# Weight parts at another remainder of 256 bytes than activations, in a two-layer trunk on one core

## The chip, the core and the metric

The kernel runs on one core of a Trainium2 chip. A core has a matrix engine (TensorE: PE in the profile, its weight loads PEld), a vector engine (VectorE, DVE), a scalar engine (ScalarE, ACT), GpSimd (POOL) and a queue engine (SyncE, SP) that here only starts transfers. Operands lie in SBUF, an on-chip memory of 128 partitions; an address in this document is a byte offset within each partition. A matmul loads a 128 x 128 block (the stationary operand, `LDWEIGHTS` in the profile) and then passes another block of 128 rows and up to 512 columns through it (the moving operand, `MATMUL`); the result goes to PSUM. The metric is the time of one execution in microseconds, the median of several runs.

## What is computed

Two decoder layers on a sequence of 512 tokens, width 2048, in float32: a retention layer (8 heads) and a latent attention layer (16 heads), each behind an RMS norm that is scaled and shifted by a conditioning vector, each with a gate path, then a last RMS norm.

```python
def reference(x, c, positions, ada_w, ada_b, norm_g, ret_w_in, ...):
    c_act = jax.nn.silu(c)
    for i in range(DEPTH):                      # DEPTH = 2
        mod = (c_act @ ada_w[i] + ada_b[i])[:, None, :]
        shift, scale, gate = jnp.split(mod, 3, axis=-1)
        h = rmsnorm(x, norm_g[i]) * (1.0 + scale) + shift
        if i % N_MIXERS == 0:
            y = retention_branch(h, positions, ...)    # (silu(g) * y) @ w_out
        else:
            y = mla_branch(h, positions, ...)          # (silu(g) * o) @ w_out
        x = x + gate * y
    return rmsnorm(x, final_norm_g)
```

## The kernel before

**Parts.** Every float32 operand of the large products is split in two tiles of a faster matmul type: a high part (ACT copies it into the type) and a low part (DVE subtracts the high part from the original). One product is then three matmuls: high by high, high by low, low by high. In the profile `vg_03o_h` and `vg_03o_l` are the two parts of one weight tile. Nearly all of the 11,100 matmul records are of this type.

**Stages, in order of time.** The opening forms the normed input `hT` and the first head's q, k, v and gate together (line 409). Then, head by head for the retention layer: v and gate weights of heads 1 to 7 (`vg`, lines 806 to 808, `seven_steps`), and between them q and k of heads 2 to 5 (`qk_..`, line 905, `seven_rows_steps`); q and k of heads 1, 6 and 7 go through `mm3` (lines 163 to 165). The retention itself runs beside the output projection (`o`, line 1387). The second layer has a gate product (`g`, lines 163 to 165 and 1651), the latent rows (`vgc`, `seven_steps` again), two gate groups (`g_..`, line 905 again), attention with its up-projections (`uq`, `uk`, `uv`, `a`, `o<-pt,v`), and the last projection (`o_w`, lines 163 to 165 and 2309).

**Which side the weights are on.** In `seven_steps` (function `product`, line 801 on) and in the first head's `v`, the block of the activations is loaded and the weights, 512 columns wide, move. Everywhere else that `whi` and `wlo` tiles are used, the weights are loaded and the activations move, 512 columns wide in most stages and 256 wide in the two `seven_rows_steps` families, in line 1651 and in the last halves of the output projections. A `seven_steps` block has 8 steps of 4 forms and 8 of 3, each form 2 x 3 matmuls: 336 matmuls; a `seven_rows_steps` group has 4 steps of 4 forms and 4 of 3, each form 12 matmuls: also 336.

**Where tiles lie.** The pool `base` is open all the time. A tile without a tag, or a tag with all its buffers, gets its place when its first tile is created, each new one behind the last. The pools `l0`, `lp`, `l1`, `l2` follow one another in the space behind `base`. Sizes are rounded to 32 bytes. The memory map of the kernel before is:

| what | first address | remainder of 256 |
|---|---|---|
| `ident`, `mask`, `ones`, `mhalf`, `rt` | 4224 | 128 for the first |
| `spacer` (32 bytes) | 5824 | 192 |
| `vcol` (736 bytes) | 5856 | 224 |
| `a_col0`, `a_col1`, `b_col0`, `b_col1`, `gate_c0`, `gate_c1` (64 bytes each) | 6592 | 192 for the first |
| `big` (16 tiles of 4096: `hT`, `h2`, inputs of the output projections, heads' q, k, v) | 6976 | 64 |
| `small` (24 of 32) | 72512 | 64 for the first |
| `k4` (8), `k4b` (4), `tmp` (6 of 2048), `raw` (3): `sums` 0 to 11, latent parts, staging | 73280 | 64 |
| `whi` (3), `wlo` (3): high and low parts of most weights | 147008 | 64 |
| `qn_s`, `mod_c` | 171584 | 64 |
| pools `lp`, `l1`, `l2` begin | 171776 | 0 |
| `lp`: `sums` 12 to 15 (activations) | 188160 | 0 |
| `lp`: `own_h`, `own_l` (weights) | 204544 | 0 |
| `l2`: `bm` (weights in `vgc` and `g_..`) | 220928 | 0 |

All these large tiles have row lengths that are multiples of 512 bytes, and every matmul operand starts at a multiple of 512 bytes within its tile, so an operand has its tile's remainder of 256.

`turns` (line 782 on) deals the weight tiles out: of every four pairs of parts, three are in `whi`/`wlo` and one in the pool's own tiles. With the counts of this kernel the own tiles always get the same steps: `vg_01o`, `03o`, `05o`, `07o`, `11e`, `13e`, `15e`, `17e`, and `qk_01o`, `03o`, `11e`, `13e`. The `sums` 12 to 15 serve the forms s and y of steps 6 and 7 (of `vg`; steps 3 of `qk`).

**Order.** The order of instructions on each engine is written out by hand (`queued`, `behind`); the change leaves it as it is.

Of the kernel before, what the change touches and what calls it, by code (L numbers as in the profile page):

```python
# [9 lines left out]
F32 = mybir.dt.float32  # L10
# [6 lines left out]
P = 128  # L17
T = 512
NT = T // P
D = 2048  # L20
KD = D // P
# [28 lines left out]
def hybrid_trunk_kernel(  # L50
# [26 lines left out]
    PE, ACT, DVE, POOL = nc.tensor, nc.scalar, nc.vector, nc.gpsimd  # L77
# [5 lines left out]
    base = ctx.enter_context(tc.tile_pool(name="base", bufs=1))  # L83
# [38 lines left out]
    mhalf = base.tile([P, NT], F32, name="mhalf")  # L122
    DVE.memset(mhalf, -0.5)
    rt = base.tile([P, 4], F32, name="rt")
    spacer = base.tile([P, 8], F32, name="spacer")
    DVE.memset(spacer, 0.0)

    def rsqrt(src, n, mul, name):

# [91 lines left out]
    gate_bias = (vcol[:, 136:152], vcol[:, 152:168])  # L221
    final_c = vcol[:, 168:184]

    a_col = [base.tile([P, KD], F32, name=f"a_col{i}") for i in range(2)]
    b_col = [base.tile([P, KD], F32, name=f"b_col{i}") for i in range(2)]
    gate_c = [base.tile([P, KD], F32, name=f"gate_c{i}") for i in range(2)]

    def modulate(i, ps_shift, ps_scale, k0, n):

# [193 lines left out]
    @contextmanager  # L423
    def behind(*engines):

        with ExitStack() as stack:
            for e in engines:
                ins = next((i for i in reversed(nc.cur_bb.bb.instructions) if i.engine == e), None)
                if ins is not None:
                    stack.enter_context(tc.issue_after(ins))  # L430
            yield

    def queued(fn, *args):
        with behind(A_, V_, T_, S_):
            return fn(*args)
# [186 lines left out]


    queued(sum_mod, 0, 0, 1)
    low_v = queued(prepares["v", 0])
    for half in range(2):
        queued(sum_mod, 0, 1, half)
# [154 lines left out]
    def turns(raw_tags, part_tags):  # L782

        n = [0, 0]

        def raw_tile(shape, name):
            n[0] += 1
            pool, tag, bufs = raw_tags[n[0] % len(raw_tags)]
            return pool().tile(shape, F32, tag=tag, bufs=bufs, name=f"{name}_r")

        def part_tiles(shape, name):
            n[1] += 1
            pool, tags, bufs = part_tags[n[1] % len(part_tags)]
            return [pool().tile(shape, F32R, tag=tag, bufs=bufs, name=f"{name}_{p}") for p, tag in zip("hl", tags)]

        return raw_tile, part_tiles
# [943 lines left out]
            DVE.tensor_add(latent["q"][2 + b], m4[b], y_[b])  # L1740
            DVE.tensor_add(latent["kv"][2 + b], m5[b], y_[b])

    qn_s = base.tile([P, 16], F32, name="qn_s")[:, :NT]

    def latent_norm(n):
        if n == "q":
# [410 lines left out]
    for i, step in enumerate(steps):  # L2157
# [8 lines left out]
        with behind(S_):  # L2166
# [3 lines left out]
            if i in (n_p, n_l2):  # L2170
                pool, tables, n0 = (pools["l1"], rotary, 0) if i == n_p else (pools["l2"], rotary2, 2)
# [301 lines left out]
```

## Time and profile before

| | us |
|---|---|
| median of 3 runs | 2152.52 |
| lowest and highest | 2151.73, 2153.0 |
| the profiled execution | 2153.75 |
| its span, first to last instruction | 2151.9 |

The profile is of one execution. Busy time of PE is the time in which at least one matmul record is open; matmuls overlap in the records, so that what a matmul costs in a row of matmuls is the step from its start to the start of the next. Where the text needs that step it is taken from the timeline: the starts of the first matmul and of the matmul behind the last, divided by the number between them. A name such as `z<-vg_03o_h,hT` reads: written tile, then the moving operand and the loaded one in the order of their names; `x2` behind a row is two matmuls merged in one row.

### The profile page before, as it was taken

Reading aid. Unit: us, or ns where it says so; the run is one execution under the profiler, and the core shown is the slowest. Engines: PE = TensorE matmul, PEld = TensorE weight load, DVE = VectorE, ACT = ScalarE, POOL = GpSimd, SP = SyncE. Lnnn points to the kernel's source line nnn. Section 1 sums busy time; section 2 is a strip of 40 time slices with the busy share of each in tenths; the row PEclk is TensorE's granted clock in tenths of the full one; section 3 lists DMA queues with packets and bytes.
Section 4 is the critical chain, followed back from the end, with each engine's and each line's share of the span. In section 5 each row is a group of like instructions: output and inputs, shape, how many; then the busy total and the mean of one; then the engine's idle time right before and its main releaser. Section 6 shows DMA issues by size and latency. Waiting matters only on the chain.

```text
span 2151.9 us, 30042 instructions
## 1 busy us (share of the span) xinstructions
PE 2128.1 (99%) x11100; PEld 1822.9 (85%) x11100; DVE 1675.4 (78%) x2482; ACT 1056.5 (49%) x1604; POOL 106.8 (5%) x178
## 2 busy tenths in 40 slices
PE   8999999999999999999999999999999999999998
PEld 5888898988889888888888888898889989888887
DVE  7898788888878789766777787667978788886745
ACT  5764444444444444434444435345446565664434
POOL 1010000000000000000000000010001000000000
PEclk9999999999999999999999999999999999999999
DMA  9975687877777778755646566553556544346734
GB/s 388 398 279 192 218 277 226 277 238 261 256 259 259 232 231 288 250 193 177 244 148 239 188 212 246 166 174 112 166 181 211 185 129 147 117 134 222 243 108 137
DMA packets 229783, 462.96 MB, mean 215 GB/s; under 512 B 20818, under 2 KB 84338, under 8 KB 225794
## 3 DMA queue, kind: packets, MB, share of 16 engines
q1 hardware_dynamic: 217424, 421.85, 59.5%
q0 software_dynamic: 11920, 38.91, 4.6%
q8 instruction: 87, 1.43, 0.3%
q14 instruction: 62, 0.50, 0.1%
q10 hardware_dynamic: 290, 0.27, 0.0%
HBM read 417.96 MB, written 43.00 MB: 214 GB/s over the span
## 4 chain that ended last, share of the span: by engine, by line
PE 84%; DVE 6%; DMA 5%; issue 2%; ACT 2%; POOL 1%; SPq 0%; DVEq 0%; POOLq 0%; ACTq 0%
PE o L1387 11%; PE o L2309 4%; PE y L807 2%; PE y L806 2%; PE y L808 2%; PE s L807 2%; PE s L806 2%; PE x L807 2%; PE x L806 2%; PE s L808 2%; PE x L808 2%; PE x_qk L905 2%; PE s_qk L905 2%; PE y_qk L905 2%; PE qk L165 2%
## 5 line engine op out<-in xcount | busy, mean ns | idle before, releaser
L1387 PE MATMUL o<-o_h,o_whi 128*128 128x512 f32 (+1 forms) x496 | 192.3, 388 | 0.0
L1387 PE MATMUL o<-o_h,o_wlo 128*128 128x512 f32 (+1 forms) x496 | 192.1, 387 | 0.2 <-DVE o_wlo L138 0.2
L1387 PE MATMUL o<-o_l,o_whi 128*128 128x512 f32 (+1 forms) x496 | 191.4, 386 | 0.0
L1387 PEld LDWEIGHTS o<-o_h,o_wlo 128*128 128x128 f32 x496 | 93.1, 188 | 20.8 <-DVE o_wlo L138 2.0
L138 DVE TENSOR_TENSOR o_wlo<-o_r,o_whi 128x1024 fp32r<-128x1024 f32 x61 | 74.5, 1223 | 44.9 <-ACT o_whi L137 41.4
L1387 PEld LDWEIGHTS o<-o_l,o_whi 128*128 128x128 f32 x496 | 93.2, 188 | 18.4
L1387 PEld LDWEIGHTS o<-o_h,o_whi 128*128 128x128 f32 x496 | 93.2, 188 | 18.1
L165 PE MATMUL qk<-hT,qk_l 128*128 128x512 f32 x192 | 75.5, 393 | 1.5 <-DVE qk_l L138 1.5
L163 PE MATMUL qk<-hT,qk_h 128*128 128x512 f32 x192 | 75.8, 395 | 0.0
L164 PE MATMUL qk<-hT,qk_h 128*128 128x512 f32 x192 | 75.2, 392 | 0.0
L1089 DVE SCALAR_TENSOR_TENSOR mod<-mod,c_odd 128x1024 f32<-128x1024 f32 x48 | 58.0, 1220 | 21.4 <-DMA mod<-in_ada_t_dram 21.4
L358 DVE SCALAR_TENSOR_TENSOR aw<-aw,c_all 128x2048 f32<-128x2048 f32 (+1 forms) x35 | 73.1, 2102 | 1.8 <-DMA aw<-in_ada_t_dram 1.6
L137 ACT CAST o_whi<-o_r 128x1024 fp32r<-128x1024 f32 x61 | 63.5, 1051 | 22.4 <-PE o L1387 14.3
L138 DVE TENSOR_TENSOR o_w_lo<-o_w_raw,o_w_hi 128x1024 fp32r<-128x1024 f32 x32 | 38.9, 1219 | 33.3 <-ACT o_w_hi L137 33.2
L1089 DVE SCALAR_TENSOR_TENSOR mod<-mod,c_bm 128x1024 f32<-128x1024 f32 x48 | 58.5, 1218 | 0.0
L2309 PE MATMUL o<-o_h,o_w_hi 128*128 128x512 f32 (+1 forms) x160 | 55.6, 348 | 0.0
L2309 PE MATMUL o<-o_h,o_w_lo 128*128 128x512 f32 (+1 forms) x160 | 55.5, 347 | 0.0
L2309 PE MATMUL o<-o_l,o_w_hi 128*128 128x512 f32 (+1 forms) x160 | 55.4, 347 | 0.0
L1242 ACT ACTIVATE yn<-y,nmr,gn_r 128x512 f32<-128x512 f32 x32 | 22.3, 778 | 62.0 <-DVE nmr L1236 62.0
L137 ACT CAST o_w_hi<-o_w_raw 128x1024 fp32r<-128x1024 f32 x32 | 33.5, 1050 | 36.9 <-PE o L2309 33.1
L164 PE MATMUL o<-o_l,o_w_hi 128*128 128x512 f32 x128 | 50.0, 391 | 0.7 <-DVE o_l L138 0.6
L137 ACT CAST o_h<-o_in 128x1024 fp32r<-128x1024 f32 x24 | 25.2, 1051 | 51.3 <-PE o L164 47.6
(1608 smaller groups left out, 6893.4 us busy)
## 6 DMA issues: line engine op xcount, KB each, us to landing
mod<-in_ada_t_dram SPq DMA_DIRECT2D x96, 512.0 KB, 6.0
o_r<-in_ret_w_out_dram SPq DMA_DIRECT2D x64, 512.0 KB, 5.3
aw<-in_ada_t_dram SPq DMA_DIRECT2D x30, 1024.0 KB, 8.9
mod_gate<-in_ada_t_dram SPq DMA_DIRECT2D x32, 512.0 KB, 5.4
o_w_raw<-in_mla_w_out_dram SPq DMA_DIRECT2D x32, 512.0 KB, 4.0
qk_r<-in_ret_w_in_dram SPq DMA_DIRECT2D x48, 256.0 KB, 3.1
qk_r<-qk_d SPq DMA_DIRECT2D x32, 256.0 KB, 5.5
v_r<-v_d SPq DMA_DIRECT2D x32, 256.0 KB, 6.1
```

The costliest lines, as they stand in the source:

```text
L137: ACT.copy(hi, src)
L138: DVE.tensor_sub(lo, src, hi.bitcast(F32))
L163: PE.matmul(o, lhs[0], rhs[0], start=first and not seeded, stop=False, skip_group_check=seeded)
L164: PE.matmul(o, lhs[0], rhs[1], start=False, stop=False, skip_group_check=seeded)
L165: return PE.matmul(o, lhs[1], rhs[0], start=False, stop=last, skip_group_check=seeded)
L806: PE.matmul(banks[b], a[0], w[0], start=first, stop=False, skip_group_check=True)
L807: PE.matmul(banks[b], a[0], w[1], start=False, stop=False, skip_group_check=True)
L808: PE.matmul(banks[b], a[1], w[0], start=False, stop=True, skip_group_check=True)
L905: PE.matmul(o, w[wp][:, i, b * P : (b + 1) * P], a[ap], start=first and i + b + k == 0, stop=k == 2, skip_group_check=True,)
L1089: DVE.scalar_tensor_tensor(out=aw, in0=aw, scalar=1.0, in1=silu_c[j], op0=ALU.mult, op1=ALU.mult, accum_out=mc[:, j, b : b + 1],)
L1387: PE.matmul(o, w[i][:, ki, c0 + b * P : c0 + (b + 1) * P], a[j], start=first and i + j == 0, stop=last and i == 1, skip_group_check=True,)
L2309: PE.matmul(banks2[b][:, cols], w[0][i][:, 0, b * P : (b + 1) * P], o2_moving(w, u, cols)[j], start=u + i + j == 0, stop=u == KD - 1 and i ...
```

## The change

The diff moves tiles; it adds and removes no work but one small fill.

```diff
@@ -122,8 +122,6 @@
     rt = base.tile([P, 4], F32, name="rt")
-    spacer = base.tile([P, 8], F32, name="spacer")
-    DVE.memset(spacer, 0.0)
@@ -221,9 +219,9 @@
-    a_col = [base.tile([P, KD], F32, name=f"a_col{i}") for i in range(2)]
-    b_col = [base.tile([P, KD], F32, name=f"b_col{i}") for i in range(2)]
-    gate_c = [base.tile([P, KD], F32, name=f"gate_c{i}") for i in range(2)]
+    a_col = [base.tile([P, KD], F32, name="a_col0")]
+    b_col = [base.tile([P, KD], F32, name="b_col0")]
+    gate_c = []
@@ -622,6 +620,8 @@
     queued(sum_mod, 0, 0, 1)
+    gate_c.extend(base.tile([P, KD], F32, name=f"gate_c{i}") for i in range(2))
+    b_col.append(base.tile([P, KD], F32, name="b_col1"))
     low_v = queued(prepares["v", 0])
@@ -791,6 +791,8 @@ def turns(raw_tags, part_tags)
             pool, tags, bufs = part_tags[n[1] % len(part_tags)]
+            if pool() is not base and len(n) == 2:
+                n.append(pool().tile([P, 48], F32, name=f"{name}_gap"))
             return [pool().tile(shape, F32R, tag=tag, bufs=bufs, name=f"{name}_{p}") for p, tag in zip("hl", tags)]
@@ -1740,7 +1742,8 @@
-    qn_s = base.tile([P, 16], F32, name="qn_s")[:, :NT]
+    a_col.append(base.tile([P, KD], F32, name="a_col1"))
+    qn_s = base.tile([P, 32], F32, name="qn_s")[:, :NT]
```

The spacer and five of the six small columns no longer stand ahead of `big`. Three of those columns (192 bytes) are now created between `raw` and the first `whi` tile, and a gap of 192 bytes is created ahead of `own_h` in `lp` and ahead of `bm` in `l2`. The last small column and 64 more bytes for `qn_s` stand behind `wlo`.

## The prediction

> **What bounds the kernel now.** First the page: span, busy time, granted clock, and the chain that ended last; then PE's own waits.
>
> ```profile
> span 2151.9 us, 30042 instructions
> PE 2128.1 (99%) x11100; PEld 1822.9 (85%) x11100; DVE 1675.4 (78%) x2482; ACT 1056.5 (49%) x1604; POOL 106.8 (5%) x178
> PEclk9999999999999999999999999999999999999999
> PE 84%; DVE 6%; DMA 5%; issue 2%; ACT 2%; POOL 1%; SPq 0%; DVEq 0%; POOLq 0%; ACTq 0%
> ...
> PE xT_ps L435 <- DVE x_diag L525: 2.7, 3, 1.7
> PE o L1387 <- DVE o_wlo L138: 0.2, 1, 0.2
> ```
>
> PE is open 99% of the span at full clock, and its longest wait, in the opening, is 2.7 us; line 1387, the costliest, waits 0.2 in all. So the time is the number of matmuls times the step from one start to the next, and the change can act only through that step or by making PE wait. The windows by stage say where PE has cover:
>
> ```profile
> 23.00:160.00 137.00, 132.08 (x577) 107.64 (x576) 123.89 (x134) 94.03 (x155) 5.19 (x10) 1.00 0.91 355
> 207.00:284.00 77.00, 77.00 (x338) 63.18 (x337) 58.74 (x73) 35.90 (x43) 2.72 (x6) 1.00 0.75 241
> 284.00:324.00 40.00, 40.00 (x337) 39.95 (x336) 35.12 (x46) 18.93 (x23) 3.60 (x7) 1.00 0.84 278
> 1015.00:1423.00 408.00, 406.91 (x1883) 337.21 (x1882) 301.30 (x487) 179.68 (x271) 12.64 (x18) 1.00 0.61 210
> 1622.00:1705.00 83.00, 83.00 (x706) 82.92 (x705) 66.35 (x89) 49.21 (x75) 5.79 (x7) 1.00 0.60 182
> ```
>
> Columns: window, length, busy PE, PEld, DVE, ACT, POOL, clock, DMA share. Only the opening (23 to 160) leaves PE idle, 5 us, with DMA at 0.91. In the 256-wide stage (284 to 324) DVE has 35.1 of 40 us to do: PE could be quicker by 12% before DVE decides.
>
> **The step depends on where the two operands lie.** The kernel before already holds all three cases, because own tiles and `sums` 12 to 15 stand at remainder 0 and all else at 64. The timeline of PE, 512 wide, weights moving:
>
> ```profile
> 223.84 0.39 PE L806 MATMUL x<-vg_03e_h,hT 128*128 128x512 f32 x1
> ...
> 226.56 0.39 PE L806 MATMUL z<-vg_03o_h,hT 128*128 128x512 f32 x1
> ...
> 229.36 0.39 PE L806 MATMUL x<-vg_04e_h,hT 128*128 128x512 f32 x1
> ...
> 277.38 0.39 PE L806 MATMUL y<-vg_16e_h,sums 128*128 128x512 f32 x1
> ...
> 280.13 0.39 PE L806 MATMUL x<-vg_17o_h,hT 128*128 128x512 f32 x1
> ```
>
> Twelve matmuls lie between each pair. Both at 64: 2.72 us, 226.7 ns each. Moving weights in an own tile, 64 below the loaded `hT` or `sums`: 2.80 us, 233.3. The third pair (weights in `whi` at 64, the loaded `sums` 12 to 15 at 0) has the moving operand 64 above the loaded one: 2.75 us, 229.2. 256 wide, weights loaded, activations moving:
>
> ```profile
> 289.98 0.40 PE L905 MATMUL x_qk<-hT,qk_01e_h 128*128 128x256 f32 x2
> ...
> 292.86 0.39 PE L905 MATMUL z_qk<-hT,qk_01o_h 128*128 128x256 f32 x2
> ...
> 295.58 0.40 PE L905 MATMUL x_qk<-hT,qk_02e_h 128*128 128x256 f32 x2
> ...
> 305.62 0.40 PE L905 MATMUL z_qk<-hT,qk_03o_h 128*128 128x256 f32 x2
> ...
> 307.03 0.40 PE L905 MATMUL x_qk<-hT,qk_10o_h 128*128 128x256 f32 x2
> ```
>
> 24 matmuls with both at 64: 2.88 us, 120.0 ns. 24 with the loaded weights 64 below the moving activations (`qk_01o`): 2.72 us, 113.3. The same relation in `qk_03o`, where the forms ahead of it had another: 12 in 1.41 us, 117.5. The levels 113.3, 120.0 and 226.7, 233.3 are 6.7 ns apart; I call that one step.
>
> [...]
>
> **What the change does to the map.** Ahead of `big`, 32 bytes of spacer and four times 64 of columns go: 6976 - 288 = 6688, remainder 32. All activations of `base`, with `k4`, `k4b`, `tmp`, `raw`, go to 32. Then 192 bytes come ahead of `whi`: 147008 - 96 = 146912, remainder 224, which is 64 below 32. Behind `wlo`, 128 more: the pools begin at 171808, remainder 32, so `sums` 12 to 15 join the other activations. The gaps put `own_h`, `own_l` and `bm` at 224. So wherever these weights are loaded, the moving activations stand 64 above; wherever they move, they stand 64 below. Weights in `k4b` and `big` tiles (the opening's gate, `uk`, `uv`, parts of both tails) move with the activations and keep their step.
>
> **The terms.** Stage lengths come from the boundaries:
>
> ```profile
> 207.42 0.39 PE L806 MATMUL x<-vg_00e_h,hT 128*128 128x512 f32 x1
> ...
> 284.24 0.40 PE L905 MATMUL x_qk<-hT,qk_00e_h 128*128 128x256 f32 x2
> ...
> 324.16 0.39 PE L806 MATMUL x<-vg_00e_h,hT 128*128 128x512 f32 x1
> ```
>
> (1) *Moving weights, 64 below.* A `vg` block takes 284.24 - 207.42 = 76.82 us for 336 matmuls; 12 of its 56 forms are in own tiles already. All at 233.3 ns: 78.40, so 1.58 more. Seven heads and `vgc`: 8 x 1.58 = **+12.6**. Bounds: the other unequal price, 229.2, would make it 8 x 0.19 = +1.5; one step above 233.3 would add 18. The own tiles are this very case, so I take 233.3.
>
> (2) *Loaded weights, 256 wide.* A `qk` group takes 39.92 us; 336 x 113.3 ns = 38.08, so 1.84 less; four heads and the two gate groups: 6 x 1.84 = **-11.0**. The tails and line 1651 have 144 + 48 + 96 = 288 more such matmuls: 288 x 6.7 ns = **-1.9**. DVE's 35.1 us and DMA's 0.84 x 40 = 33.6 us fit under 38.1. At the 117.5 of `qk_03o` the two would be 6 x 0.44 = 2.6 and 0.7, together -3.3 in place of -12.9: +9.6 on the sum. I take 113.3, as in the change no form with another relation precedes within a group.
>
> (3) *Loaded weights, 512 wide.* These rows carry most of PE, three matmuls each row's kind:
>
> ```profile
> L1387 PE MATMUL o<-o_h,o_whi 128*128 128x512 f32 x480 | 187.8, 391 | 0.0
> L163 PE MATMUL qk<-hT,qk_h 128*128 128x512 f32 x192 | 75.8, 395 | 0.0
> L163 PE MATMUL o<-o_h,o_w_hi 128*128 128x512 f32 x128 | 50.1, 391 | 0.0
> L163 PE MATMUL g<-h,g_h 128*128 128x512 f32 x104 | 40.5, 389 | 0.0
> L163 PE MATMUL uq<-qT,uq 128*128 128x512 f32 x96 | 37.5, 391 | 0.0
> L2309 PE MATMUL o<-o_h,o_w_hi 128*128 128x512 f32 x96 | 37.3, 389 | 0.0
> ...
> L163 PE MATMUL o<-pt,v 128*128 128x512 f32 x16 | 6.4, 398 | 0.0
> ```
>
> 3 x (480 + 192 + 128 + 104 + 96 + 96) = 3288, and 192 in the opening (q and k of head 0): 3480. No row of before has this case 512 wide; the nearest is `vg_16e` with `sums`, the same relation of moving to loaded operand with the roles exchanged, 229.2. At 2.5 ns each 3288 cost +8.2; the opening's 192 hide under its DMA. **+8.2.** Bounds: one step either way from 226.7, as the 256-wide form gained one and `vg_03o` lost one: -22 to +22.
>
> (4) *The rest.* The opening's 192 matmuls with moving `v` weights cost 6.6 ns each, 1.3 us, mostly under its DMA: +0.4. `o<-pt,v` (48 of 512 columns): `pt` moves from 0 to 32 and so to `v`'s remainder, away from the 64 below that it has now: -0.3. The removed fill is 0.07 us near the start, ahead of any matmul; splits and copies move with their tiles:
>
> ```profile
> 0.97 0.07 DVE L126 MEMSET spacer<- 128x8 f32 x1
> ...
> L841 DVE TENSOR_TENSOR vg_03o_l<-vg_03o_r,vg_03o_h 128x1024 fp32r<-128x1024 f32 x1 | 1.2, 1226 | 0.4 <-ACT vg_03o_h L840 0.4
> L838 DVE TENSOR_TENSOR vg_03e_l<-vg_03e_r,vg_03e_h 128x1024 fp32r<-128x1024 f32 x1 | 1.2, 1217 | 0.0
> ```
>
> A split at remainder 0 takes 1226 ns and one at 64 takes 1217: under 1%, on an engine with 22% idle. Zero; were DVE the bound in the 256-wide stage, 1% of its 35 us would be 0.4 us a head. The tiles' order of creation adds no wait: the columns are written long after.
>
> **Sum.** 12.6 - 11.0 - 1.9 + 8.2 + 0.4 - 0.3 = +8.0. Against the profiled execution's 2153.75 that is 2161.8; that execution was 1.2 above the median of the runs, so I say 2152.5 + 8.0 = 2160.5.
>
> **The rivals.** *Within 0.2%* (4.3 us, about what a measurement can tell from no change): term 3 stays at 226.7. Sum -0.2: 2152.3. For it: no row has the case itself, and 2.5 ns are a third of a step. Against: the 12 matmuls of `vg_16e` average 229.2. That the map isn't what I worked out (another tile is created earlier than I read) ends here too.
>
> *Faster.* The 512-wide matmuls with loaded weights gain one step, as the 256-wide ones did: 3288 x -6.7 ns = -22 in place of +8.2, sum -22, 2130. It decides once term 3 is under -4.1 us, a step below 225.4 ns. For it: it is the same relation and the same roles as in `qk_01o`. Against: `vg_16e`, same relation, same width, no gain.
>
> *Slower by more.* Remainders 32 and 224 are no multiples of 64, and no row of before has such an operand. If the levels come in pieces of 64 bytes (226.7 ns / 512 is 0.44 ns a column, so 6.7 ns are 15 columns, some 60 bytes), a row that starts within a piece touches one more: one step on each of some 10,700 matmuls, +72, 2232. Against: nothing in the trace speaks of absolute remainders; `qk_03o` and `qk_01o` differ though theirs are equal. [...] Milder: the 256-wide groups stay at 117.5, sum +17.6, 2170.
>
> **How the numbers follow.** Forecast 0.44 (its own range 2157 to 2168), 117.5 in the 256-wide groups 0.08 (2170), the 64-byte pieces 0.10 (2185 to 2232, as not every matmul need pay): slower 0.62. Within 0.2%: 0.20. Faster: 0.18, of which half between 2143 and 2148, since not all of the 3288 need gain. The range leaves out the far half of the faster case and most of the 64-byte case: 2143 to 2186.
>
> **What would show it.** In the profile after, `z<-vg_00o_h` should rise from the step 226.7 to that of `vg_03o`, 233.3, a `vg` block from 76.8 to 78.4 us, a `qk` group fall from 39.9 to 38.1, and 24 matmuls of line 1387 take 5.50 us in place of 5.44. PE's waits should stay under 2 us a stage. A `vg` block of 76.8 or less, or line 1387 at 220 or 233 ns, would make the prediction wrong.

## The result, and the profile after

The kernel after takes 2168.99 us (median of 4 runs, 2168.24 to 2169.81) against 2152.76 (4 runs, 2151.73 to 2153.93): 16.2 us slower, ratio 1.0078, 95% interval 1.0065 to 1.0091. The forecast was 8.0 us slower. (The kernel before was run again beside each experiment below, with medians of 2151.3 to 2152.1 us; each ratio is against the runs beside it.) The profiled execution's span is 2167.1 us against 2151.9, so 15.2 us have to be found; the profiled execution of before was about 1 us above the median. Of the six small columns the diff moves four, as the prediction's sum has it, and not five: `a_col0` and `b_col0` stay ahead of `big`. First the page after: span, PE, clock, and the shares of the chain that ended last.

```profile
span 2167.1 us, 30041 instructions
PE 2141.6 (99%) x11100; PEld 1817.1 (84%) x11100; DVE 1675.9 (77%) x2481; ACT 1055.4 (49%) x1604; POOL 106.5 (5%) x178
PEclk9999999999999999999999999999999999999999
PE 83%; DVE 6%; DMA 6%; issue 2%; ACT 2%; POOL 1%; SPq 0%; POOLq 0%; DVEq 0%; ACTq 0%
```

DVE and ACT are as busy as before (1675.9 and 1055.4 against 1675.4 and 1056.5 us), the clock is full (1.00 in its windows below), and the same 11,100 matmuls keep PE open 13.5 us longer. The waits of PE after, their sum, count and longest:

```profile
PE xT_ps L433 <- DVE x_diag L523: 3.2, 4, 1.4
PE c_ps L433 <- DMA c_all<-in_c_dram: 3.1, 1, 3.1
...
PE qk L163 <- DVE qk_l L136: 1.5, 1, 1.5
```

Nothing new: the two over 2 us lie in the opening, as before. The time went into the step from one matmul to the next. Now the windows of four stages, before and then after: a `vg` block, a `qk` group, the product `o` with the retention beside it, the two gate groups. Columns as in the prediction (window, length, busy PE, ...).

```profile
207.42:284.24 76.82, 76.82 (x338) 63.03 (x337) 58.81 (x72) 35.90 (x43) 2.68 (x6) 1.00 0.75 241
284.24:324.16 39.92, 39.92 (x338) 39.92 (x336) 34.88 (x46) 18.93 (x23) 3.52 (x7) 1.00 0.84 279
1016.34:1422.90 406.56, 405.47 (x1876) 336.04 (x1875) 300.92 (x486) 179.10 (x270) 12.09 (x17) 1.00 0.61 209
1622.28:1705.12 82.84, 82.84 (x706) 82.84 (x704) 66.19 (x89) 49.29 (x75) 5.91 (x7) 1.00 0.60 183
```

```profile
208.17:286.56 78.39, 78.39 (x337) 62.83 (x336) 59.74 (x74) 35.88 (x43) 2.70 (x6) 1.00 0.76 243
286.56:326.14 39.58, 39.58 (x338) 39.57 (x337) 34.87 (x46) 18.87 (x23) 3.43 (x7) 1.00 0.82 273
1027.86:1435.40 407.54, 406.82 (x1875) 336.52 (x1874) 301.08 (x486) 178.97 (x270) 12.06 (x17) 1.00 0.61 209
1636.95:1719.61 82.66, 82.66 (x706) 82.65 (x705) 66.38 (x89) 49.27 (x75) 6.34 (x7) 1.00 0.60 183
```

A `vg` block is 1.57 us longer, to the forecast's 78.4. A `qk` group is 0.34 shorter where 1.84 had been forecast. The whole `o` stage is 1.0 longer. Two short windows of after show the steps; the line ahead of them is line 1387 of before:

```profile
1060.02:1065.46 5.44, 5.44 (x26) 4.50 (x25) 2.57 (x5) 2.03 (x4) 0.00 (x0) 1.00 0.86 272
```

```profile
1072.14:1077.63 5.49, 5.49 (x26) 4.50 (x24) 2.16 (x4) 2.25 (x5) 0.00 (x0) 1.00 0.93 295
292.22:295.04 2.82, 2.82 (x26) 2.82 (x25) 2.79 (x5) 0.13 (x1) 0.00 (x0) 1.00 0.99 343
```

All three hold 24 matmuls (the counts take in those that overlap an edge). Line 1387 of before: 5.44 us, 226.7 ns each. Line 1389, which is the same line in the kernel after: 5.49 us, 228.9 ns each, as forecast. A `qk` group: 2.82 us, some 117.5 ns (117.8 over the whole group), not 113.3.

Both traces have the same matmuls in the same order, so the difference between their starts can be summed by kind:

| term of the prediction | forecast, us | measured, us |
|---|---|---|
| (1) moving weights: `vg` 10.80, `vgc` 1.56 | +12.6 | +12.4 |
| (2) 256 wide, `qk` and gate groups: -1.40, -0.19 | -11.0 | -1.6 |
| (2) 256 wide, tails of `o` and `o_w`, line 1653: -0.25, -0.53, -0.09 | -1.9 | -0.9 |
| (3) 512 wide, loaded: `o` 1.27, `o_w` 0.93, `g` 0.62, `uq` 0.28, q and k -0.03 | +8.2 | +3.1 |
| (4) opening | +0.4 | +1.5 |
| (4) `o<-pt,v` | -0.3 | -0.3 |
| everything else | 0 | +0.5 |

That makes 14.7; the other 0.5 of the 15.2 lies ahead of the first matmul and behind the last.

### The profile page after: what moved, and what is told of

Same layout as the page of the kernel before. It is cut to its first block, busy times and chain, and to the rows that moved or that the text cites. A ratio compares the mean times of both kernels' runs of the same rounds, so it can differ in the third digit from the quotient of the medians.

```text
span 2167.1 us, 30041 instructions
## 1 busy us (share of the span) xinstructions
PE 2141.6 (99%) x11100; PEld 1817.1 (84%) x11100; DVE 1675.9 (77%) x2481; ACT 1055.4 (49%) x1604; POOL 106.5 (5%) x178
## 4 chain that ended last, share of the span: by engine, by line
PE 83%; DVE 6%; DMA 6%; issue 2%; ACT 2%; POOL 1%; SPq 0%; POOLq 0%; DVEq 0%; ACTq 0%
PE o L1389 9%; PE o L2312 4%; PE y L810 2%; PE s L808 2%; PE y L808 2%; PE x L810 2%; PE s L810 2%; PE x L808 2%; PE y L809 2%; PE s L809 2%; PE x L809 2%; PE y_qk L907 2%; PE s_qk L907 2%; PE x_qk L907 2%; PE qk L163 2%
## 5 line engine op out<-in xcount | busy, mean ns | idle before, releaser
L161 PE MATMUL o<-o_h,o_w_hi 128*128 128x512 f32 x128 | 50.5, 395 | 0.0
```

The lines of the kernel that those rows point to most:

```text
L161: PE.matmul(o, lhs[0], rhs[0], start=first and not seeded, stop=False, skip_group_check=seeded)
```

## The experiments

Two theories stood at the start. **The relation**: the step depends on where the moving operand lies against the next loaded one, modulo 256, and 256 wide it also depends on what ran before. **The place**: remainders 32 and 224, or these tiles, are slow by themselves.

**e1: the relation by itself.** A kernel of nothing but groups of matmuls, with DVE, ACT and DMA idle. `group` takes the count, the columns, and the offsets of the moving and the loaded operand in elements of 4 bytes:

```diff
+    for n in (512, 256):
...
+        for d in range(0, 64, 4):
+            group(24, n, 0, 0)
+            group(48, n, d, 0)
+            group(24, n, 0, 16)
+            group(48, n, d, 0)
...
```

> This kernel leaves the whole computation out: it loads one block of x, splits nothing, and runs groups of 48 float32r matmuls (the kernel's triples: first weights with two moving tiles, second weights with the first) with the moving operand placed d bytes above the loaded one, d from 0 to 240 in steps of 16, 512 and 256 columns wide, each d once behind 24 matmuls at d = 0 and once behind 24 with the moving operand 64 below; then groups with both operands shifted by 16, 32 or 48 bytes. Theory (only the relation modulo 256 and the step that ran before count): 512 wide 226.7 ns at d = 0, 229 at 64, 233.3 at 192; 256 wide 120.0 at 0, and at 64 113.3 behind d = 0 but 117.7 behind 64 below; shifting both by 16, 32 or 48 changes nothing. Rival (absolute remainders, 64-byte pieces): both shifted by 16, 32 or 48 costs about 6.7 ns a matmul more at d = 0. Rival (neighbouring traffic of DVE, ACT and DMA makes the levels): without any such traffic all d take the same step.

Mean step in ns over the second half of each group of 48, behind equal operands / behind the moving one 64 below:

| d, bytes | 512 wide | 256 wide | d, bytes | 512 wide | 256 wide |
|---|---|---|---|---|---|
| 0 | 226.7 | 120.0 | 128 | 233.5 / 233.2 | 118.6 / 118.6 |
| 16 | 231.6 / 231.6 | 118.7 / 116.6 | 144 | 233.4 / 233.3 | 118.6 / 118.6 |
| 32 | 233.3 / 233.3 | 117.7 / 117.7 | 160 | 234.3 / 234.6 | 117.4 / 117.5 |
| 48 | 233.3 / 233.4 | 118.3 / 118.4 | 176 | 231.0 / 231.3 | 119.2 / 119.4 |
| 64 | 228.9 / 233.4 | 117.7 / 113.4 | 192 | 233.4 / 233.3 | 113.3 / 113.4 |
| 80 | 230.9 / 231.3 | 120.1 / 119.9 | 208 | 234.6 / 234.8 | 119.1 / 119.1 |
| 96 | 233.2 / 233.1 | 119.8 / 119.8 | 224 | 233.3 / 233.4 | 118.2 / 118.3 |
| 112 | 231.4 / 230.8 | 113.4 / 113.4 | 240 | 233.4 / 236.8 | 117.4 / 117.1 |

Some of these groups as windows: 512 wide at d = 0 (72 matmuls), 64, 192, and d = 0 with both shifted by 16 and by 32; then 256 wide at d = 0 (72), 64 behind equal operands, and 64 behind 64 below.

```profile
44.36:60.71 16.35, 16.35 (x73) 13.51 (x72) 0.00 (x0) 0.00 (x0) 0.00 (x0) 1.00 0.00 1
160.95:171.96 11.01, 11.01 (x49) 9.01 (x48) 0.00 (x0) 0.00 (x0) 0.00 (x0) 1.00 0.00 0
...
427.89:439.08 11.19, 11.19 (x49) 8.98 (x48) 0.00 (x0) 0.00 (x0) 0.00 (x0) 1.00 0.00 0
561.92:572.96 11.04, 11.04 (x49) 8.99 (x48) 0.00 (x0) 0.00 (x0) 0.00 (x0) 1.00 0.01 1
578.43:589.35 10.92, 10.92 (x50) 9.01 (x48) 0.00 (x0) 0.00 (x0) 0.00 (x0) 1.00 0.00 0
689.09:697.73 8.64, 8.64 (x74) 8.64 (x73) 0.00 (x0) 0.00 (x0) 0.00 (x0) 1.00 0.01 2
748.64:754.30 5.66, 5.66 (x50) 5.66 (x49) 0.00 (x0) 0.00 (x0) 0.00 (x0) 1.00 0.01 3
757.03:762.47 5.44, 5.44 (x50) 5.44 (x49) 0.00 (x0) 0.00 (x0) 0.00 (x0) 1.00 0.00 0
```

The relation makes the levels, and no neighbour's traffic is needed: the columns of DVE, ACT and POOL are zero, DMA's share is 0.01, and the levels are there. With both operands unshifted, equal ones are the best case 512 wide (226.7 ns) and among the slowest 256 wide (120.0). The last two rows are the same 48 matmuls: 5.66 or 5.44 us, by what ran before them; 512 wide, the relation 64 above has two levels as well, 228.9 and 233.4. But the rule that I had written down, which relation leads to which level, came out the other way round here: 117.7 behind equal operands, 113.4 behind 64 below. The sixteen groups of 24 with the moving operand 64 below, 256 wide, settled at 113.3 nine times and at 117.8 seven times. So there are two levels for the same placement, and one relation ahead isn't enough to say which. Shifting both operands by 32 changes nothing (second half 226.7); by 16 or 48 it costs 3.4 and 4.4 ns 512 wide at d = 0 and saves 1.6 and 1.8 ns 256 wide. The rival's 64-byte pieces are gone for 32, while 16 does count, so the relation isn't the whole rule.

**e2: everything equal.**

```diff
-    spacer = base.tile([P, 8], F32, name="spacer")
-    DVE.memset(spacer, 0.0)
...
-    qn_s = base.tile([P, 16], F32, name="qn_s")[:, :NT]
+    qn_s = base.tile([P, 32], F32, name="qn_s")[:, :NT]
```

> The kernel before without its spacer and with 64 bytes more behind the weight tiles: activations, shared weights, own weights and sums 12 to 15 all at remainder 32. Theory (relation alone): no matmul has unequal operands any more; vg blocks 76.2 us (336 x 226.7 ns), qk groups 40.3 us (336 x 120.0), 24 matmuls of line 1387 5.44 us; about 3.4 + 0.8 + 0.4 us saved and 2.4 us lost, 2150.5 us. Rival (remainder 32 costs by itself and made part of the +16): line 1387 above 226.7 ns, qk above 120.0, time 2160 or more.

Measured 2149.25 us against 2151.44; ratio 0.9988, interval 0.9980 to 0.9997. The windows of the four stages:

```profile
207.76:283.92 76.16, 76.16 (x337) 63.06 (x336) 58.80 (x72) 35.89 (x43) 2.61 (x6) 1.00 0.74 242
283.92:324.23 40.31, 40.31 (x337) 40.30 (x336) 34.89 (x46) 19.01 (x23) 3.60 (x7) 1.00 0.82 276
1013.39:1418.60 405.21, 404.27 (x1877) 336.66 (x1876) 301.04 (x486) 179.11 (x270) 12.10 (x17) 1.00 0.61 210
1617.20:1701.30 84.10, 84.10 (x706) 84.10 (x704) 66.50 (x89) 49.28 (x75) 6.24 (x7) 1.00 0.59 180
```

336 x 226.7 and 336 x 120.0 ns, to within 0.01 us. Remainder 32 costs nothing by itself, and the second theory falls for it. Remainder 224 was not run with equal operands; e9 below has the same price with other remainders. The kernel before had lost 0.66 us in each `vg` block to its own tiles and `sums` 12 to 15, and gained 0.39 in each `qk` group from them.

**e3: only the own tiles back to equal**, in the kernel after:

```diff
-            if pool() is not base and len(n) == 2:
-                n.append(pool().tile([P, 48], F32, name=f"{name}_gap"))
```

> The kernel after without the gap ahead of the own tiles: own weights stand at 32 with the activations, shared weights stay at 224. Each fourth form of a qk group then runs at 120.0 ns ahead of three forms with the loaded weights 64 below. Theory (the level of 256-wide matmuls with that relation is set by what ran before: 113.3 behind equal operands, 117.7 behind moving weights 64 below): the three forms run at 113.3, a qk group takes 84 x 120.0 + 252 x 113.3 = 38.6 us against 39.6 in the kernel after, and the own forms of a vg block fall to 226.7 to 229 (0.3 to 0.5 us a block); total about 2160 us. Rival (117.7 belongs to this place of the shared tiles, whatever ran before): qk group 84 x 120.0 + 252 x 117.7 = 39.7 us, total about 2166.5 us.

Measured 2162.29 us against 2151.44, ratio 1.0048 (1.0034 to 1.0062): 6.7 us less than the kernel after. One `qk` group in windows: its first 72 matmuls, the two forms of the own tile `qk_01o` (24), the next 48, and the whole group.

```profile
286.36:294.84 8.48, 8.48 (x74) 8.48 (x73) 8.34 (x13) 3.49 (x5) 2.41 (x5) 1.00 1.01 369
294.84:297.71 2.87, 2.87 (x27) 2.87 (x25) 2.78 (x4) 1.98 (x2) 0.00 (x0) 1.00 0.46 153
297.71:303.15 5.44, 5.44 (x51) 5.44 (x49) 5.31 (x7) 3.05 (x3) 0.00 (x0) 1.00 0.53 164
...
286.36:325.23 38.87, 38.87 (x338) 38.87 (x337) 34.54 (x45) 18.90 (x23) 3.09 (x6) 1.00 0.83 276
```

This shows what the missed term lacked. Behind the `vg` block the group starts at 117.8 ns (8.48 us / 72) and stays there, form after form. The own tile with equal operands runs at 119.6 and settles at 120.0. Behind it the same relation, in the same shared tiles, runs at 113.3 (5.44 / 48) and stays there, through three more interruptions by own tiles: 72 x 117.8 + 72 x 120 + 192 x 113.3 ns = 38.88 us. The kernel after has no equal form in these groups and runs at 117.8 from the first matmul to the last. The rival's 39.7 is excluded. What the moving weights ahead have to do with it is not shown: in e3 the own tile `vg_17e` makes the last six matmuls ahead of the group equal ones, and it starts at 117.8 all the same.

**e4: the weights 64 above instead.** In e2's kernel, without the wider `qn_s`:

```diff
+    base.tile([P, 16], F32, name="gap")
     low_v = queued(prepares["v", 0])
```

> The kernel of e2 with 64 bytes ahead of the shared weight tiles, so that they stand 64 above the activations (own weights and sums 12 to 15 stay equal to the activations). Theory (the relation alone, by e1's groups): 512-wide loaded weights have the moving activations 64 below, 233.3 ns in place of 226.7, so 24 matmuls of line 1387's product take 5.60 us and 3288 of them cost about 22 us; moving weights 64 above give 229.0, a vg block 76.7 to 76.9 us; qk groups between 38.6 (113.3) and 39.7 us (117.8). Total 2166 to 2176 us. Rival (what costs is that weights and activations lie apart, not on which side): as in the kernel after, vg blocks 78.4, line 1387 5.50, about 2168 us.

Measured 2171.17 us in one run. Windows: 24 matmuls of the product `o`, a `vg` block, a `qk` group; then of this group the first 72 matmuls, and 48 behind the own tile's 24.

```profile
1072.03:1077.63 5.60, 5.60 (x26) 4.51 (x25) 4.77 (x10) 2.44 (x5) 0.00 (x0) 1.00 1.04 367
209.38:286.54 77.16, 77.16 (x338) 63.09 (x337) 58.97 (x73) 35.84 (x43) 2.68 (x6) 1.00 0.75 242
286.54:325.96 39.42, 39.42 (x337) 39.42 (x336) 34.89 (x46) 18.89 (x23) 3.47 (x7) 1.00 0.83 275
...
286.54:294.71 8.17, 8.17 (x74) 8.17 (x72) 8.06 (x12) 3.38 (x4) 2.38 (x5) 1.00 1.01 370
...
297.58:303.24 5.66, 5.66 (x51) 5.66 (x49) 5.53 (x7) 3.05 (x3) 0.00 (x0) 1.00 0.49 153
```

The roles swap as the relation says: loaded weights now have the activations 64 below, 5.60 us / 24 = 233.3 ns, and the moving weights lie above, a cheap 77.16 (0.3 over the range given); the kernel after, with the weights below, has 5.49 and 78.39. The sign matters, not the mere distance. In the group the order of the levels is the reverse of e3's: it starts at 113.5 ns (8.17 us / 72), and behind the own tile's equal forms the shared tiles run at 117.9 (5.66 / 48) and stay at 117.8 to 118.0 to the group's end. So an equal form does not always bring the fast level: behind it e3 goes on at 113.3, with the activations 64 above the weights, and e4 at 117.8, with them 64 below.

**e5 and e6: the gain alone.** e2's kernel, with the shared weights of the 256-wide groups used 192 bytes further on in larger tiles:

```diff
-        return base.tile(list(shape), F32, tag="tmp", bufs=6, name=name)
+        return base.tile(list(shape), F32, tag="tmp", bufs=5, name=name)
...
+            o = 48 if low and (not own or LOW_OWN) else 0
+            c = 1088 if not own or LOW_OWN else 1024
...
+                t = pool().tile([P, c], F32R, tag=tag, bufs=bufs, name=f"{name}_{p}")
+                v = t[:, o : o + (1024 if len(shape) == 3 else T)]
```

> The kernel of e2 (all equal) with one part of the change alone: only in the 256-wide groups (four qk heads, two gate groups) the shared weight tiles are used 192 bytes further on, which puts them 64 below the activations modulo 256; there the own tiles and the first even tile stay equal. To make room the staging tiles of tag tmp are 5 in place of 6. Theory (113.3 ns is reached when the form ahead ran with equal operands, and is kept until something breaks it): each qk group about 38.6 us against 40.3 in e2, the gate groups 3 us less together, vg blocks stay at 76.2, time about 2139 us, plus whatever the missing staging tile costs (0 to 4 us). Rival (the shared tiles keep 117.8 unless weights moved ahead of them as in e3): groups of 39.7 us, time 2146.

> As e5, but the own tiles too stand 64 below in the 256-wide groups; only the first even tile of a group stays equal. Theory (the state entered behind equal operands is kept through the group): 24 matmuls at 120.0 and 312 at 113.3, 38.2 us a qk group, time 1 to 3 us under e5. Rival (113.3 needs to be renewed by equal forms, and falls back to 117.8 at the first disturbance): groups between 38.6 and 39.6 us, time above e5.

Both missed: 2173.76 (ratio 1.0099, 1.0082 to 1.0116) and 2176.72 us (1.0117, 1.0102 to 1.0132). In e5, unlike its text, the first even tile stood 64 below too; only the own tiles were equal. Its waits of PE, then its first `vg` block, the first `qk` group, the 48 matmuls behind that group's first own tile, and a stretch within the third group:

```profile
PE y_qk L913 <- ACT g_st L714: 10.2, 4, 2.8
PE s L814 <- ACT g_st L714: 8.1, 2, 4.7
```

```profile
209.22:285.38 76.16, 76.16 (x337) 63.06 (x336) 59.55 (x74) 35.32 (x42) 2.41 (x5) 1.00 0.77 248
285.38:328.27 42.89, 39.71 (x337) 39.30 (x336) 34.54 (x45) 19.14 (x24) 3.35 (x6) 1.00 0.75 252
...
300.50:306.15 5.65, 5.65 (x50) 5.65 (x49) 5.52 (x7) 3.05 (x3) 0.00 (x0) 1.00 0.51 147
530.10:536.90 6.80, 6.18 (x29) 6.18 (x30) 4.72 (x6) 3.52 (x5) 1.08 (x2) 0.50 0.60 205
```

The staging tile was the mishap: the copies of g out of PSUM (`g_st`) have five tiles to share, and PE waits for them 18 us in all; e7, with six, has no such wait. The clock took some more: three stretches, 17 us together, show a granted clock of 0.50 as in the last line, and e2 has none at these places; the mean over the span is 0.994, against 0.998 in e2. By my estimate from the 0.50, half of the 17 is lost, 8.5 us, and less as far as PE was waiting in it anyway.

Two things of e5 bear on the level. The `vg` block ahead is all equal (76.16 us), yet the group starts at 117.8 (24 matmuls in 2.83 us): moving weights 64 below aren't needed for that. And behind the own tile's 24 equal matmuls (some 120 ns) this group went on at 117.7 (5.65 us / 48); only the next own tile brought 113.3. e6 tells something too. Its group began with 24 equal matmuls, went on at 113.3, met a step of 2.4 us within its third form, and later stood at this (48 matmuls):

```profile
296.86:302.51 5.65, 5.65 (x50) 5.65 (x49) 5.47 (x8) 3.00 (x3) 0.00 (x0) 1.00 0.47 150
```

117.7 ns: after the wait the level is the other one, and with no equal form ahead it stays so to the group's end. That is the level that e6's rival had.

**e7 and e8: the gain alone, with room.** All six buffers of `tmp` again; each shared buffer gets its 64 bytes, and small columns that exist anyway fill the 192 up to the next one. `slots.add` takes the normal start, the low start and the size in elements; the low start is used in the 256-wide groups alone:

```diff
-        return base.tile([P, n], F32, tag="small", bufs=24, name=name)
+        return base.tile([P, n], F32, tag="small", bufs=14, name=name)
...
+    slots.add("whi", 16, 0, 1040)
+    for t in (a_col, a_col, b_col):
+        t.append(base.tile([P, KD], F32, name=f"cola{len(a_col)}{len(b_col)}"))
+    slots.add("wlo", 16, 0, 1040)
...
-                st = l1_tile("st6", 4, f"st_{h}_{i}", (P, 6))
+                st = l1_tile("st6", 1, f"st_{h}_{i}", (P, 6))
```

> Everything equal as in e2 (all 512-wide matmuls at 226.7 ns), and in the 256-wide groups alone the shared weights 64 below the activations, but without e5's missing staging tile: each shared weight buffer gets its 64 bytes from columns laid between the buffers and from 10 fewer tiny statistics buffers. The first even tile of a group and the own tiles stay equal. Theory (113.3 behind equal operands, kept until a stall; e5's loss was the staging tile): PE waits in the qk groups as in e2 (none of e5's waits for the copies of g), groups of 38.6 us against 40.3, gate groups 3 us less together: 2149.2 - 6.8 - 3.0 = about 2139.5 us. Rival (the quicker groups leave PE waiting for weights, DVE or staging, and the 2.6 to 4.6 us a group that e5 lost come back here): 2150 or more.

Measured 2146.42 us against 2152.12, ratio 0.9975 (0.9966 to 0.9984). The groups did it: 38.72 us in the window below, which is 96 equal matmuls at 120.0 and 240 at 113.3. But the time is 7 us over the expectation. A new wait accounts for 3.5 of them; the rest is not accounted for:

```profile
PE s L198 <- ACT yn L1274: 5.6, 4, 1.5
```

```profile
283.10:321.82 38.72, 38.72 (x338) 38.71 (x337) 33.97 (x45) 18.91 (x24) 3.63 (x8) 1.00 0.87 292
1008.76:1417.00 408.24, 403.79 (x1875) 336.22 (x1874) 304.24 (x486) 179.06 (x270) 12.09 (x17) 1.00 0.60 208
```

In the `o` stage PE is idle 4.45 us (408.24 - 403.79) against 0.94 in e2. e8:

```diff
-                st = l1_tile("st6", 1, f"st_{h}_{i}", (P, 6))
+                st = l1_tile("st6", 2, f"st_{h}_{i}", (P, 6))
```

> As e7, but the retention stage has two tiny statistics tiles (tag st6) in place of e7's one (four in the kernel before). Theory (e7's 3.5 us in the stage of the product o, where PE waited 5.6 us for yn against 1.0 in e2, come from that one tile, which makes each bn_stats wait for the bn_aggr before it): most of it comes back, 2143 to 2144 us. Rival (they come from the 10 fewer tiles of tag small, or from the earlier arrival of the heads): no change, 2146.

Measured 2141.84 us against 2151.73, ratio 0.9955 (0.9941 to 0.9968), 1 to 2 us below the expectation. Wait and windows of e8:

```profile
PE s L198 <- ACT yn L1274: 1.6, 4, 0.5
```

```profile
283.07:321.78 38.71, 38.71 (x337) 38.70 (x336) 33.96 (x45) 18.91 (x24) 3.62 (x8) 1.00 0.88 298
1007.57:1413.90 406.33, 404.89 (x1879) 337.10 (x1878) 301.73 (x486) 179.10 (x270) 12.09 (x17) 1.00 0.61 210
```

The single statistics tile had been the wait: PE's idle time in the `o` stage falls from 4.45 to 1.44 us. This kernel is faster than the one before by 9.9 us, and than the one after by some 27.

**e9: the loss alone.** With e8's buffers, the low start in the `vg` and `vgc` blocks only:

```diff
 # in seven_steps, and so for the other parts
-                    eh, el = part_tiles([P, 2, T], f"{n}e")
+                    eh, el = part_tiles([P, 2, T], f"{n}e", True)
...
 # in seven_rows_steps, and so for the other parts
-                    eh, el = part_tiles([P, 2, T], f"{n}e", u > 0)
+                    eh, el = part_tiles([P, 2, T], f"{n}e")
...
```

> The moving part of the change alone: with the buffers of e8, the shared weights stand 64 below the activations only in the vg and vgc blocks, where weights move; in the 256-wide groups, own tiles and everything 512 wide with loaded weights all operands stay equal. Theory (the step depends on the relation alone, so the part costs the same alone as in the whole change): 264 of a block's 336 matmuls at 233.3 in place of 226.7 ns, blocks of 77.9 to 78.1 us against 76.2, qk groups 40.3, eight blocks 14 us: 2149.2 + 14 + 0 to 3.5 for the room (e7) = 2163 to 2167 us. Rival (the blocks are slow only where the rest of the kernel is unequal too): blocks of 76.2, 2150 us.

Measured 2165.61 us in one run. A `vg` block and a `qk` group:

```profile
206.44:284.54 78.10, 78.10 (x337) 62.89 (x336) 60.50 (x74) 35.59 (x43) 2.12 (x5) 1.00 0.74 242
284.54:324.86 40.32, 40.32 (x338) 40.31 (x337) 34.44 (x45) 18.80 (x24) 4.01 (x8) 1.00 0.85 284
```

Term 1's relation is enough by itself for such a loss: 78.10 - 76.16 = 1.94 us a block over e2, and 15.5 for eight. The place plays no part: with this edit the first shared buffer starts at 4224 + 736 = 4960, so the weights there have the remainder 96 and the loaded activations, 64 further, 160, where the kernel after has 224 and 32; a matmul of the shared tiles takes 233.3 ns in both.

## Why the prediction was right in direction and short by half

**Bound.** Right: PE stays busy for the whole of the `vg`, `qk` and gate windows above, and in the `o` stage for all but 0.7 us. One reading was loose: the 2.7 us named as PE's longest wait are three waits together, and the longest single one was 2.6 us, on a DMA.

**Term 1.** Right: 78.39 to 78.40 us a block, +12.4 for +12.6. It carries the result.

**Term 2 failed.** The step was: "I take 113.3, as in the change no form with another relation precedes within a group." Within the group that is so, but it doesn't give 113.3: the group starts at 117.8 and, with nothing to change the level, ends there (39.58 us for 336). e3 and e8 show what brought 113.3 in this kernel: 256-wide forms with equal operands ahead. The kernel before had it where its own tiles came behind such forms at 120.0 (`qk_01o`), and not in `qk_03o`, behind another relation; by moving every tile to the same relation, the change took away the very forms that led to the fast level. That is no general rule: in the `qk` and gate groups of e3, e5, e7 and e8, forms with the weights 64 below went on at 113.3 in 103 of the 110 places behind an equal form, and at 117.8 in seven; e4's, with the weights 64 above, went on at 117.8 to 118.0 in 25 of 25. Why a group is entered at 117.8 stays open: it is so behind 336 moving weights 64 below (the kernel after) and behind 336 equal matmuls (e5). The row for this stood in the prediction: `qk_03o` at 117.5, named as a bound and as the milder rival with 8 in 100. That rival is what happened: -3.3 forecast by it for both parts of term 2, -2.5 measured; 10.4 us of expected gain were missing. That its total of 2170 us lies so near the measured 2169.0 is luck in part, as it has term 3 at +8.2.

**Term 3 was right in the step and too large in the sum.** Line 1389 runs at 228.9 ns. But before, the mean of the undisturbed steps of these products was 226.8 to 227.0 (228.0 in `uq`), so the price is 2 ns rather than 2.5 (3.4 in q and k, 1 in `uq`). And steps longer than 250 ns, where PE stood for something, held 9.4 us above the usual step in these stages before and 5.4 after; I put that down to a slower PE, which gives its suppliers time. Together +3.1 for +8.2, which by luck hid half of term 2's miss. That the step came out at 228.9 was not certain either: e1 has this relation at 233.4 behind another one. That the shorter waits follow from the slower steps is argued, not shown by a run of its own.

**Term 4.** The opening lost 1.5 us instead of 0.4: the `v` matmuls there (192) got 1.4 longer, so the transfers don't cover them as I had thought.

**The rivals.** The faster one fell with line 1389 at 228.9, the 64-byte one with e2: equal operands at 32 take 226.7 and 120.0. e1's rival, neighbours' traffic as the maker of the levels, fell too: with DVE, ACT and POOL at zero, 512 wide, the step is 226.7 ns at d = 0 and 233.4 at 192. Why a shift of both operands by 16 bytes costs 3.4 ns there (d = 0) and one by 32 nothing, no run shows.

## What to carry to other kernels

Where matmuls run back to back and each loads new weights, note the addresses of both operands modulo 256 and read the start-to-start step per form; here equal remainders were best 512 wide (226.7 ns in e2, 228.9 and 233.3 in the kernel after) and loaded weights 64 below were better 256 wide (113.3 to 117.8, against 120.0 in e2), so one shift for both widths lost on one of them. A step that is faster in a few forms can depend on the forms ahead (113.3 in e3, behind equal ones, and 117.8 in the kernel after, which has none): before pricing a whole stage at it, ask at which level the stage is entered, what will change it, and whether the change takes that away. And when room is made for a test, check the waits of the engines that used it: one staging tile cost more here than the effect under study (18 us of waits in e5; e8 is 9.9 us faster than the kernel before), and one statistics tile 4.6 us, near half of it (e7 against e8).

## What was not expected of the hardware

The same 256-wide matmuls with the same addresses settle at 113.3 or at 117.7 ns a step and keep that level for a whole group (the kernel after: 39.58 us for 336). Equal operands settled at 120.0 in all but two of e1's unshifted groups, which took 119.7. What chooses the level beyond the form ahead stays open: in e1 the moving operand 64 below gave 113.3 nine times and 117.8 seven times, and 64 above gave 117.7 behind equal operands, where e3 and e8 have 113.3. A relation of 64 above cost 228.9 at e1's unshifted place, but 226.7 with both operands 16 bytes further on, where equal operands cost 230.1; so the relation modulo 256 is not the whole rule either.
